# One of four weight sums of a seven-product scheme: added by DVE beside the product of one of its terms, in place of an accumulating DMA

## The chip, the cores and the metric

The kernel runs on one core of one Trainium2 chip. The metric is the device time in microseconds (us) from start to end of one execution; the median of three runs stands for the kernel. Engines are named as the profile names them: PE (matrix products), PEld (its weight loads), DVE, ACT, POOL, and SP, which only issues DMAs.

## The reference

The reference is a two-layer encoder trunk on x of 256 tokens by 2048 channels in float32. Each layer normalises x, projects it by `w_in`, runs three token mixers (retention, pooling, windowed attention), and merges their outputs with gates:

```
ya = (mixer a * silu gate) @ w_ret     # likewise yb @ w_pool, yc @ w_att, each 1024 -> 2048
gates = sigmoid(h @ w_in[mg])          # 3 x 2048 columns
merged = gates[0]*ya + gates[1]*yb + gates[2]*yc
x = x + merged @ w_out
```

What the change touches is the right half (columns 1024 to 2047) of the three products by `w_att`, `w_ret` and `w_pool`.

## The kernel before

All matrix products run in float32 split in two parts: each weight tile (128x1024 float32, 512 KB) is loaded into a `raw` tile by SP (line 258; 4 buffers), ACT casts it to `whi` (line 271; 4 buffers), DVE subtracts to get the rest, `wlo` (line 282; 3 buffers), and PE makes three products: a_hi by whi, a_hi by wlo, a_lo by whi. One tile so treated is a use. `_plan` writes all uses (some 660) down in the order in which PE takes them, and `weights()` issues the casts and subtractions two to three uses ahead and the loads up to four raw tiles ahead of the last `wlo`. A full use is 12 matmuls with 512 columns on PE.

A merge branch (`merge_branch`; three in each layer, six in all, numbered 1 to 6 here) walks over 40 full uses (`MERGE_STD`): gate columns in blocks 2, 3 and 0, then the left part of the output weight, block 0 (n = 25 to 28), then gate block 1 (n = 29 to 36), then weight block 1. After the use with number n in the table `AFTER` it puts in one of seven products, P1, P2, Q5, P6, Q3, P7, Q4, by which the right half, a two by two block product in rows, columns and channels, is made from seven block products and not eight. Each has two half uses, q = 0 and 1, of 6 matmuls each (line 893), into one of two PSUM banks (`px` for P1, P6, P7, Q4 and `pv` for P2, Q5, Q3). The right operands are quarters of the output weight or sums of them. Four products take sums:

- P1, Q5, P6 and Q4 walk through a chain: one tile for each q, to which POOL adds the next quarter by an accumulating DMA (line 284) after each use.
- P7 takes quarter (0,1) plus quarter (1,1). SP loads quarter (0,1) into a fresh raw tile, and POOL issues an accumulating DMA of quarter (1,1) on top of it (line 260). The cast to `whi` waits for that. Quarter (1,1) is also, unsummed, the operand of Q3, three uses earlier in `AFTER`.

After each product the result is copied aside by ACT (`snap`, line 867) or combined by DVE into the `mrg` tiles (`part`, `mg`, `mrg`, lines 810 to 828). In branches 3 and 6 PE also transposes finished `mrg` tiles (`pmt`, line 458) between the uses of gate block 1.

The order of instructions on an engine is set by the tile framework's scheduler, from the order of the program text and the buffers. On each engine instructions run in that order.

Of the kernel before, what the change touches and what calls it, by code (L numbers as in the profile page):

```python
# [12 lines left out]
ALU = mybir.AluOpType  # L13
# [3 lines left out]
P = 128  # L17
# [20 lines left out]

MERGE_STD = (("mg", 2), ("mg", 3), ("mg", 0), ("w", 0), ("mg", 1), ("w", 1))
BRANCHES = ((2, "w_att"), (0, "w_ret"), (1, "w_pool"))  # L40
AFTER = {12: "P1", 14: "P2", 17: "Q5", 23: "P6", 26: "Q3", 29: "P7", 34: "Q4"}


def _plan():


    tiles, uses = [], []

    def tile_no(name, l, rows, c0, w):
        tiles.append((name, l, rows, c0, w))  # L50
        return len(tiles) - 1

    def n_tiles(name, l, c0, nk):
        return [(name, l, [k2 * 256, k2 * 256 + P], c0, 512) for k2 in range(nk // 2)]

    def t_tiles(l, c0):
        return [("w_in", l, [(k4 * 4 + i) * P for i in range(4)], c0, 256) for k4 in range(KD // 4)]

    def use(ts):
        uses.extend(("tile", tile_no(*t)) for t in ts)  # L60

    def pool_tiles(l, g2):
        use([("pool_w", l, [g2 * 512 + i * P for i in range(4)], 0, 256)])

    def merge(l, b, name, late_pool):

        quarter = {}
        for i in range(2):
            for j in range(2):
                for q in range(2):  # L70
                    quarter[i, j, q] = tile_no(name, l, [(4 * q + 2 * kk + i) * P for kk in range(2)], 1024 + 512 * j, 512)
        n = 0
        for what, c in MERGE_STD:
            ts = n_tiles("w_in", l, OFF["mg"] + b * D + c * 512, KD) if what == "mg" else n_tiles(name, l, c * 512, KW)
            for t in ts:
                use([t])
                n += 1
                for q in range(2) if n in AFTER else ():
                    stage = {"P1": 0, "Q5": 1, "P6": 2, "Q4": 3}
                    prod = AFTER[n]  # L80
                    if prod in stage:
                        st = stage[prod]
                        uses.append(("chain", (l, b, q), st, quarter[((0, 0), (0, 1), (1, 1), (1, 0))[st] + (q,)],
                                     None if st == 3 else quarter[((0, 1), (1, 1), (1, 0))[st] + (q,)]))
                    elif prod == "P7":
                        uses.append(("sum", quarter[0, 1, q], quarter[1, 1, q]))
                    else:
                        uses.append(("tile", quarter[1, 0 if prod == "P2" else 1, q]))
            if what == "mg" and c == 2 and late_pool:
                pool_tiles(l, 1)  # L90

    for l in range(DEPTH):
        use(n_tiles("w_in", l, OFF["akv"], KD))
        for j in range(2):
            use(n_tiles("w_in", l, OFF["aq"] + j * 512, KD))
        for j in range(4):
            use(t_tiles(l, OFF["ag"] + j * 256))
        for h in range(RH):
            use(t_tiles(l, OFF["rq"] + h * RD) + t_tiles(l, OFF["rk"] + h * RD))
        for part in ("rv", "rg"):  # L100
            for j in range(2):
                use(n_tiles("w_in", l, OFF[part] + j * 512, KD))
        merge(l, *BRANCHES[0], False)
        for g in range(4):
            use(t_tiles(l, OFF["pv"] + g * 256))
        for g in range(4):
            use(t_tiles(l, OFF["pg"] + g * 256))
            if g == 2:
                pool_tiles(l, 0)
        merge(l, *BRANCHES[1], True)  # L110
        merge(l, *BRANCHES[2], False)
        for c in range(4):
            use(n_tiles("w_out", l, c * 512, KD))
    return tiles, uses
# [39 lines left out]
def kernel(  # L154
# [18 lines left out]
    nc = tc.nc  # L173
# [8 lines left out]
    def nm(s):  # L182
        uid[0] += 1
        return f"{s}_{uid[0]}"
# [46 lines left out]
    tiles, uses = _plan()  # L231
# [4 lines left out]
    def tile_of(n):  # L236
        _, _, rows, _, w = tiles[n]
        return [P, len(rows), w], weight_tiles[n].rearrange("p (k e) -> p k e", k=len(rows))

    def load_to(n):  # L240
        while len(raws) < min(n, len(uses)):
            i = len(raws)
            kind = uses[i][0]
            if kind == "chain":
                _, key, stage, no, _ = uses[i]
                if stage == 0:
                    shape, src = tile_of(no)
                    chains[key] = slot(shape, F32, "chain")
                    nc.sync.dma_start(out=chains[key], in_=src)
                raws.append(chains[key])  # L250
                continue
            shape, src = tile_of(uses[i][1])
            raw = wp.tile(shape, F32, tag="raw", name=nm("raw"), bufs=N_RAW)
            if i == 0:
                for k in range(shape[1]):
                    nc.sync.dma_start(out=raw[:, k], in_=src[:, k])
            else:
                nc.sync.dma_start(out=raw, in_=src)
            if kind == "sum":
                nc.gpsimd.dma_start(out=raw, in_=tile_of(uses[i][2])[1], accum_op=ALU.add)  # L260
            raws.append(raw)

    def hi_to(n):
        while len(his) < min(n, len(uses)):
            i = len(his)
            hi = wp.tile(list(raws[i].shape), F32R, tag="whi", name=nm("whi"), bufs=N_HI)
            if i == 0:
                for k in range(hi.shape[1]):
                    nc.vector.tensor_copy(hi[:, k], raws[i][:, k])
            else:  # L270
                nc.scalar.copy(hi, raws[i])  # L271
            his.append(hi)
# [14 lines left out]
    def weights():  # L287

        i = used[0]
        used[0] += 1  # L290
        ahead = min(i, 1) if i < 6 else N_LO - 1
        hi_to(i + ahead + 1)
        lo_to(i + ahead + 1)
        load_to(len(los) + N_RAW)
        hi_to(i + ahead + (1 if ahead < N_LO - 1 else 2))
        return his[i], los[i]
# [256 lines left out]
    for l in range(DEPTH):  # L553
# [305 lines left out]
        def merge_branch(which, ut, late_pool=None):  # L859
# [11 lines left out]
                    merged[c] = slot([P, 2, 512], F32, "mrg")  # L871
                done[c, t] = start(corner_task(first, c, t, gates, op, a, b))

            def product(name):
                if name == "P1":
                    state["x"] = bank("m0", "px")
                if name in ("P2", "Q5"):
                    state["v"] = bank("m1", "pv")
                acc_ = state["x"] if name in ("P1", "P6", "P7", "Q4") else state["v"]
                fresh = name in ("P1", "P2", "Q5")  # L880
                for q in range(2):
                    hi, lo = weights()
                    for kk in range(2):
                        j = 2 * q + kk
                        if name in ("P1", "P2", "Q4"):
                            i, t = {"P1": (0, 0), "P2": (1, 0), "Q4": (1, 1)}[name]
                            u = need(ut[j])
                            a = [u[:, i, h, t * P:(t + 1) * P] for h in range(2)]
                        else:
                            u = need(combos[j])  # L890
                            a = [u[:, ("Q5", "P6", "P7", "Q3").index(name), h] for h in range(2)]
                        for n, (ah, w) in enumerate(((a[0], hi), (a[0], lo), (a[1], hi))):
                            nc.tensor.matmul(acc_, lhsT=ah, rhs=w[:, kk], start=fresh and q == 0 and kk == 0 and n == 0,  # L893
                                             stop=q == 1 and kk == 1 and n == 2, skip_group_check=not fresh)
                if name == "P1":
                    snap("p1", acc_)
                elif name == "P2":
                    corner(2, 0, ALU.add, acc_, snaps["p1"])
                elif name == "Q5":
                    snap("q5", acc_)  # L900
                elif name == "P6":
                    snap("u2", acc_)
                elif name == "Q3":
                    corner(3, 0, ALU.subtract, acc_, snaps["u2"])
                elif name == "P7":
                    snap("u3", acc_)
                    corner(3, 1, ALU.subtract, snaps["q5"], snaps["u3"])
                else:
                    corner(2, 1, None, acc_, None)

            def between():
                state["n"] += 1
                if state["n"] == COMBOS_AT:
                    combos.extend(start(combos_task(j, ut, combos)) for j in range(4))
                if state["n"] in AFTER:
                    product(AFTER[state["n"]])

            for what, c in MERGE_STD:
                if what == "mg":
# [233 lines left out]
```

## Time and profile before

| | us |
|---|---|
| median of 3 runs | 1833.59 (1832.61 to 1835.93) |
| profiled execution | 1830.8 |
| its span | 1829.0 |
| PE busy in it | 1800.4 |
| DVE busy | 1206.9 |
| ACT busy | 917.6 |
| mean granted PE clock | 0.995 of full speed |

PE is busy in 98% of the span. The ends of matmuls in the profile are modelled and overlap, so the distance between the starts of two matmuls is the better measure of what one takes. The interval of the span not covered by PE is 28.6 us.

### The profile page before, as it was taken

How to read it: one execution, taken by the hardware profiler on the slowest of the kernel's cores; microseconds unless marked ns; L12 is line 12 of the kernel's file. 1: busy time of each engine (PE TensorE's matmuls, PEld its weight loads, DVE VectorE, ACT ScalarE, POOL GpSimd, SP SyncE). 2: the span in 40 equal slices, each digit the busy share in tenths (PEclk: the TensorE clock that was granted, in tenths of full speed). 3: DMA queues.
4: the chain of work that ended last, by engine and by line, in shares of the span. 5: the costliest groups of instructions: out<-in, count | busy, mean ns of one | idle time of the engine just before them, and what ended most of it. 6: DMA issues, size and time to landing. Idle time of an engine off the chain costs nothing.

```text
span 1829.0 us, 23536 instructions
## 1 busy us (share of the span) xinstructions
PE 1800.4 (98%) x8794; PEld 1512.3 (83%) x8794; DVE 1206.9 (66%) x1554; ACT 917.6 (50%) x1171; POOL 60.2 (3%) x70
## 2 busy tenths in 40 slices
PE   9999999999999999999999999999999999999999
PEld 7888888887888878878888888888878888788787
DVE  6778765755777666655567778657657776765654
ACT  6455554554445544544444555545544455444442
POOL 0000000000000000000000000000100000001000
PEclk9999999999999999999999999999999999999999
DMA  9554455586556876865565544556865568768654
GB/s 318 196 196 161 158 166 184 185 251 208 187 200 200 242 225 207 232 188 176 185 196 184 188 163 160 172 177 204 233 207 191 200 207 231 229 211 232 188 194 150
DMA packets 103011, 364.99 MB, mean 200 GB/s; under 512 B 11888, under 2 KB 12528, under 8 KB 102896
## 3 DMA queue, kind: packets, MB, share of 16 engines
q1 hardware_dynamic: 95264, 337.37, 54.9%
q0 software_dynamic: 6912, 25.17, 7.7%
q8 instruction: 69, 1.13, 0.2%
q10 hardware_dynamic: 720, 0.94, 0.2%
q14 instruction: 46, 0.38, 0.1%
HBM read 361.34 MB, written 2.10 MB: 199 GB/s over the span
## 4 chain that ended last, share of the span: by engine, by line
PE 92%; DMA 5%; issue 1%; DVE 1%; ACT 0%; ACTq 0%; SPq 0%; DVEq 0%; POOLq 0%
PE pn L384 58%; PE pt L430 16%; PE pt L433 8%; DMA raw<-in_weight_tiles_dram 4%; PE px L893 4%; PE pv L893 2%; DVE wlo L282 1%; ACT whi L271 0%; DMA xt<-in_x_t_dram 0%; PE pmt L458 0%; PE ppt L458 0%; PE pqt L458 0%; PE py L465 0%; PE pro L465 0%; PE pss L465 0%
## 5 line engine op out<-in xcount | busy, mean ns | idle before, releaser
L282 DVE TENSOR_TENSOR wlo<-raw,whi 128x1024 fp32r<-128x1024 f32 x615 | 750.8, 1223 | 492.3 <-PE pn L384 302.6
L271 ACT CAST whi<-raw 128x1024 fp32r<-128x1024 f32 x615 | 645.6, 1052 | 649.4 <-PE pn L384 364.7
L384 PE MATMUL pn<-whi,ht 128*128 128x512 f32 x2424 | 751.6, 391 | 0.8 <-ACT ht L483 0.5
L384 PEld LDWEIGHTS pn<-whi,ht 128*128 128x128 f32 x2424 | 454.8, 188 | 95.2 <-ACT ht L483 0.9
L384 PE MATMUL pn<-wlo,ht 128*128 128x512 f32 x1212 | 460.4, 390 | 1.2 <-DVE wlo L282 1.1
L430 PE MATMUL pt<-ht,whi 128*128 128x512 f32 x1280 | 449.5, 396 | 0.0
L433 PE MATMUL pt<-ht,wlo 128*128 128x256 f32 x1280 | 353.2, 281 | 0.0
L430 PEld LDWEIGHTS pt<-ht,whi 128*128 128x128 f32 x1280 | 238.6, 188 | 53.5
L384 PEld LDWEIGHTS pn<-wlo,ht 128*128 128x128 f32 x1212 | 228.0, 188 | 48.7 <-DVE wlo L282 2.3
L433 PEld LDWEIGHTS pt<-ht,wlo 128*128 128x128 f32 x1280 | 241.5, 189 | 3.2
L384 PE MATMUL pn<-whi,mt 128*128 128x512 f32 x512 | 158.4, 392 | 0.0
L384 PEld LDWEIGHTS pn<-whi,mt 128*128 128x128 f32 x512 | 96.1, 188 | 19.9
L384 PE MATMUL pn<-wlo,mt 128*128 128x512 f32 x256 | 97.0, 389 | 0.0
L282 DVE TENSOR_TENSOR wlo<-chain,whi 128x1024 fp32r<-128x1024 f32 x48 | 58.7, 1224 | 47.4 <-PE pn L384 39.9
L271 ACT CAST whi<-chain 128x1024 fp32r<-128x1024 f32 x48 | 50.7, 1056 | 52.8 <-PE pn L384 50.3
L384 PEld LDWEIGHTS pn<-wlo,mt 128*128 128x128 f32 x256 | 48.1, 188 | 9.7
L284 POOL DMA_DIRECT2D chain<-in_weight_tiles_dram x36 | 31.6, 877 | 736.3 <-DVE wlo L282 697.6
L893 PE MATMUL px<-whi,uo 128*128 128x512 f32 x96 | 37.7, 452 | 13.9 <-ACT whi L271 13.9
L448 ACT COPY tb<-pt 128x512 f32<-128x512 f32 x40 | 23.4, 585 | 54.5 <-PE pt L430 54.3
L924 ACT ACTIVATE mg<-pn,rstd 128x512 f32<-128x512 f32 x48 | 30.4, 686 | 37.1 <-PE pn L384 37.1
L384 PE MATMUL pn<-whi,utr 128*128 128x512 f32 x128 | 39.1, 389 | 0.0
L384 PE MATMUL pn<-whi,uta 128*128 128x512 f32 x128 | 39.1, 389 | 0.0
(216 smaller groups left out, 1458.1 us busy)
## 6 DMA issues: line engine op xcount, KB each, us to landing
raw<-in_weight_tiles_dram SPq DMA_DIRECT2D x615, 512.0 KB, 3.4
chain<-in_weight_tiles_dram POOLq DMA_DIRECT2D x36, 512.0 KB, 5.4
chain<-in_weight_tiles_dram SPq DMA_DIRECT2D x12, 512.0 KB, 4.3
raw<-in_weight_tiles_dram POOLq DMA_DIRECT2D x12, 512.0 KB, 8.9
xa<-in_x_dram SPq DMA_DIRECT2D x4, 512.0 KB, 6.6
out_dram<-o SPq DMA_DIRECT2D x7, 256.0 KB, 4.7
xt<-in_x_t_dram SPq DMA_DIRECT2D x5, 256.0 KB, 6.1
lag<-in_c_lag_dram SPq DMA_DIRECT2D x2, 512.0 KB, 4.6
```

Source lines behind the costliest of these rows:

```text
L271: nc.scalar.copy(hi, raws[i])
L282: nc.vector.tensor_sub(lo, raws[i], his[i].bitcast(F32))
L284: nc.gpsimd.dma_start(out=raws[i], in_=tile_of(uses[i][4])[1], accum_op=ALU.add)
L384: nc.tensor.matmul(pt[t] if early else pt[:, t, :], lhsT=a2[:, kk, ai, ts], rhs=w[:, kk], start=k2 == 0 and n == 0, stop=k2 == n2 - 1 and ...
L430: nc.tensor.matmul(pt[:, e, :], lhsT=hi[:, kk, es], rhs=a.rearrange("p h n -> p (h n)"), start=start, stop=stop)
L433: nc.tensor.matmul(pt[:, e, 0:S], lhsT=lo[:, kk, es], rhs=a[:, 0, :], start=False, stop=False)
L448: nc.scalar.copy(b, pt[:, :, S:2 * S])
L893: nc.tensor.matmul(acc_, lhsT=ah, rhs=w[:, kk], start=fresh and q == 0 and kk == 0 and n == 0, stop=q == 1 and kk == 1 and n == 2, skip_gr ...
L924: nc.scalar.activation(g, pt[:, t], AF.Sigmoid, scale=sc(t))
```

## The change

Q3 and P7 both come after n = 27, and their half uses alternate: Q3 q0, P7 q0, Q3 q1, P7 q1. P7 still loads quarter (0,1) into a fresh raw tile, but in place of the accumulating DMA DVE adds to it the raw tile of the use just before, which is the Q3 half use with the same q and holds quarter (1,1). That makes 12 DVE additions of 128x1024 float32 and 12 fewer accumulating DMAs of 512 KB in the whole kernel (two for each of six branches). The number of matmuls, casts and subtractions is the same. What followed each of the two products (copy, combination) follows both.

```diff
-AFTER = {12: "P1", 14: "P2", 17: "Q5", 23: "P6", 26: "Q3", 29: "P7", 34: "Q4"}
+AFTER = {12: ("P1",), 14: ("P2",), 17: ("Q5",), 23: ("P6",), 27: ("Q3", "P7"), 34: ("Q4",)}
...
                     elif prod == "P7":
-                        uses.append(("sum", quarter[0, 1, q], quarter[1, 1, q]))
+                        uses.append(("sum", quarter[0, 1, q]))
...
                 nc.sync.dma_start(out=raw, in_=src)
-            if kind == "sum":
-                nc.gpsimd.dma_start(out=raw, in_=tile_of(uses[i][2])[1], accum_op=ALU.add)
             raws.append(raw)
...
             hi = wp.tile(list(raws[i].shape), F32R, tag="whi", name=nm("whi"), bufs=N_HI)
+            if uses[i][0] == "sum":
+                nc.vector.tensor_tensor(raws[i], raws[i], raws[i - 1], ALU.add)
             if i == 0:
...
-                if state["n"] in AFTER:
-                    product(AFTER[state["n"]])
+                names = AFTER.get(state["n"], ())
+                for q in range(2):
+                    for name in names:
+                        half_product(name, q)
+                for name in names:
+                    product_done(name)
```

`half_product` is the body of the old `product` for one q; `product_done` is its tail (copy or combination).

On DVE in branch 1, before: raw_3688 and raw_3706 are Q3's tiles, raw_3718 is n = 27, raw_3732 is n = 28, raw_3756 is n = 29, raw_3774 is P7's q0 (its q1 follows three rows on).

```order
L282 TENSOR_TENSOR wlo_3730<-raw_3669,whi_3720 128x1024
L282 TENSOR_TENSOR wlo_3754<-raw_3688,whi_3734 128x1024
L282 TENSOR_TENSOR wlo_3772<-raw_3706,whi_3758 128x1024
L282 TENSOR_TENSOR wlo_3791<-raw_3718,whi_3777 128x1024
L282 TENSOR_TENSOR wlo_3804<-raw_3732,whi_3796 128x1024
L282 TENSOR_TENSOR wlo_3817<-raw_3756,whi_3808 128x1024
L828 TENSOR_TENSOR part_3835<-pv_3571,u_726_3728 128x512
L810 TENSOR_TENSOR mrg_3816<-part_3835,mg_3547 128x512
L282 TENSOR_TENSOR wlo_3838<-raw_3774,whi_3821 128x1024
```

The same place now: raw_3688 is n = 27, raw_3706 and raw_3732 are Q3's tiles, raw_3718 and raw_3756 are P7's, raw_3774 is n = 28.

```order
L281 TENSOR_TENSOR wlo_3730<-raw_3669,whi_3720 128x1024
L281 TENSOR_TENSOR wlo_3754<-raw_3688,whi_3734 128x1024
L265 TENSOR_TENSOR raw_3718<-raw_3718,raw_3706 128x1024
L281 TENSOR_TENSOR wlo_3772<-raw_3706,whi_3758 128x1024
L265 TENSOR_TENSOR raw_3756<-raw_3756,raw_3732 128x1024
L281 TENSOR_TENSOR wlo_3791<-raw_3718,whi_3776 128x1024
L281 TENSOR_TENSOR wlo_3809<-raw_3732,whi_3795 128x1024
L281 TENSOR_TENSOR wlo_3822<-raw_3756,whi_3813 128x1024
L281 TENSOR_TENSOR wlo_3834<-raw_3774,whi_3826 128x1024
```

Each addition stands in DVE's row one place ahead of the subtraction of the half use before its own. The second stands ahead of two subtractions, `wlo_3791` and `wlo_3809`, that do not need it.

On DVE in branch 3, before, from the combination of Q3 (`part_6695`) to that of P7 (`part_6785`), with the two `mrg_3752` rows that finish the left block 0:

```order
L828 TENSOR_TENSOR part_6695<-pv_6433,u_1277_6590 128x512
L812 TENSOR_TENSOR mg_6409<-part_6695,mg_6409 128x512
L813 TENSOR_TENSOR mrg_3816<-mrg_3816,mg_6409 128x512
L282 TENSOR_TENSOR wlo_6699<-raw_6635,whi_6681 128x1024
L812 TENSOR_TENSOR mg_6610<-pn_6614,mg_6610 128x512
L812 TENSOR_TENSOR mg_6612<-pn_6614,mg_6612 128x512
L282 TENSOR_TENSOR wlo_6718<-raw_6654,whi_6703 128x1024
L813 TENSOR_TENSOR mrg_3752<-mrg_3752,mg_6610 128x512
L282 TENSOR_TENSOR wlo_6736<-raw_6667,whi_6722 128x1024
L282 TENSOR_TENSOR wlo_6748<-raw_6679,whi_6740 128x1024
L813 TENSOR_TENSOR mrg_3752<-mrg_3752,mg_6612 128x512
```

The same place now, where wlo_6721 is of n = 30 and wlo_6748 of n = 31:

```order
L827 TENSOR_TENSOR part_6739<-pv_6433,u_1277_6590 128x512
L281 TENSOR_TENSOR wlo_6721<-raw_6672,whi_6711 128x1024
L811 TENSOR_TENSOR mg_6409<-part_6739,mg_6409 128x512
L827 TENSOR_TENSOR part_6743<-q_1254_6458,u_1305_6719 128x512
L812 TENSOR_TENSOR mrg_3858<-mrg_3858,mg_6409 128x512
L811 TENSOR_TENSOR mg_6411<-part_6743,mg_6411 128x512
L281 TENSOR_TENSOR wlo_6748<-raw_6685,whi_6725 128x1024
L812 TENSOR_TENSOR mrg_3858<-mrg_3858,mg_6411 128x512
L811 TENSOR_TENSOR mg_6610<-pn_6614,mg_6610 128x512
L811 TENSOR_TENSOR mg_6612<-pn_6614,mg_6612 128x512
L812 TENSOR_TENSOR mrg_3752<-mrg_3752,mg_6610 128x512
L812 TENSOR_TENSOR mrg_3752<-mrg_3752,mg_6612 128x512
```

The combination of P7 has moved ahead of the last four rows, which finish `mrg_3752`.

On PE in branch 3, before, from the end of P7 to the first transpose of `mrg_3752`:

```order
L893 MATMUL px_6264<-wlo_6718,uo_6383 128x512
L893 MATMUL px_6264<-whi_6703,uo_6383 128x512
L384 MATMUL pn_6717<-whi_6722,ht_144 128x512
...
L384 MATMUL pn_6717<-wlo_6736,ht_144 128x512
L384 MATMUL pn_6717<-whi_6722,ht_144 128x512
L458 MATMUL pmt_6780<-ident,mrg_3752 128x128 x4
```

The same place now:

```order
L891 MATMUL px_6264<-wlo_6683,uo_6383 128x512
L891 MATMUL px_6264<-whi_6674,uo_6383 128x512
L383 MATMUL pn_6614<-whi_6687,utp_5215 128x512
...
L383 MATMUL pn_6747<-whi_6699,ht_134 128x512 x4
...
L383 MATMUL pn_6747<-wlo_6721,ht_144 128x512
L383 MATMUL pn_6747<-whi_6711,ht_144 128x512
L457 MATMUL pmt_6784<-ident,mrg_3752 128x128 x4
```

The transpose stands after the matmuls of n = 30 in both. Before, one full use lay between the last matmul of P7 and it, now three do (n = 28, 29 and 30).

## Rows read from the trace of the kernel before

**Rows 1.** The page: busy time of each engine over the span.

```profile
PE 1800.4 (98%) x8794; PEld 1512.3 (83%) x8794; DVE 1206.9 (66%) x1554; ACT 917.6 (50%) x1171; POOL 60.2 (3%) x70
```

**Rows 2.** Groups by shape: count, busy us, mean ns, idle ahead and its releaser.

```profile
L893 PE MATMUL px<-whi,uo 128*128 128x512 f32 x96 | 37.7, 452 | 13.9 <-ACT whi L271 13.9
L893 PE MATMUL pv<-whi,uo 128*128 128x512 f32 x96 | 31.5, 389 | 0.0
...
L893 PE MATMUL px<-wlo,uo 128*128 128x512 f32 x48 | 22.5, 469 | 6.3 <-DVE wlo L282 6.3
```

**Rows 3.** Chain that ended last, branch 1, Q5 to Q4: start, length, what.

```profile
380.59 2.72 PE pv L893 x12
...
399.63 2.72 PE px L893 x12
...
411.63 3.18 DMA raw<-in_weight_tiles_dram
...
415.43 8.80 DMA raw<-in_weight_tiles_dram
...
441.72 2.72 PE px L893 x12
```

**Rows 4.** Same chain, branches 2 to 6: start of Q5, then of Q4.

```profile
608.37 2.72 PE pv L893 x12
...
671.45 2.72 PE px L893 x12
...
742.17 2.72 PE pv L893 x12
...
807.71 2.72 PE px L893 x12
...
1290.89 2.72 PE pv L893 x12
...
1352.62 2.72 PE px L893 x12
...
1519.27 2.72 PE pv L893 x12
...
1580.68 2.72 PE px L893 x12
...
1651.40 2.72 PE pv L893 x12
...
1715.93 2.72 PE px L893 x12
```

**Rows 5.** Same chain, branch 3 behind P7: two uses with a transpose block between.

```profile
796.31 2.75 PE pn L384 x12
799.50 8.21 PE pn L384 x36
```

**Rows 6.** Stretch of P7 in branch 3: length, busy and count by engine, PE clock.

```profile
786.00:792.00 6.00, 5.02 (x11) 3.61 (x12) 5.53 (x7) 4.21 (x5) 0.00 (x0) 0.55 0.40 131
```

**Rows 7.** The page's DMA issues: queue, count, size, median us to landing.

```profile
raw<-in_weight_tiles_dram SPq DMA_DIRECT2D x615, 512.0 KB, 3.4
...
raw<-in_weight_tiles_dram POOLq DMA_DIRECT2D x12, 512.0 KB, 8.9
```

**Rows 8.** Line 258's four loads behind P6: branch 1 (395:408), then branch 2 (622:636).

```profile
DMA to landing us min/median/max: 3.2/4.1/4.2
...
DMA to landing us min/median/max: 4.6/4.8/4.9
```

**Rows 9.** DVE in order of time, branch 1: start, length, idle ahead and its releaser.

```profile
404.94 1.23 DVE L282 TENSOR_TENSOR wlo<-raw,whi 128x1024 fp32r<-128x1024 f32 x1 [1.50 <-PE pn L384]
...
414.24 0.68 DVE L828 TENSOR_TENSOR part<-pv,u 128x512 f32<-128x512 f32 x1
```

**Rows 10.** The page's costliest groups: DVE's subtraction and ACT's cast.

```profile
L282 DVE TENSOR_TENSOR wlo<-raw,whi 128x1024 fp32r<-128x1024 f32 x615 | 750.8, 1223 | 492.3 <-PE pn L384 302.6
L271 ACT CAST whi<-raw 128x1024 fp32r<-128x1024 f32 x615 | 645.6, 1052 | 649.4 <-PE pn L384 364.7
```

More of the change, by code (lines that the diff above doesn't have):

```diff
@@ L77, in merge @@
                 n += 1
-                for q in range(2) if n in AFTER else ():
+                for q, prod in [(q, prod) for q in range(2) for prod in AFTER.get(n, ())]:
                     stage = {"P1": 0, "Q5": 1, "P6": 2, "Q4": 3}
-                    prod = AFTER[n]
                     if prod in stage:
@@ L872, in corner, with half_product @@
                 done[c, t] = start(corner_task(first, c, t, gates, op, a, b))
-            def product(name):
-                if name == "P1":
+            def half_product(name, q):
+                if name == "P1" and q == 0:
                     state["x"] = bank("m0", "px")
-                if name in ("P2", "Q5"):
+                if name in ("P2", "Q5") and q == 0:
                     state["v"] = bank("m1", "pv")
@@ L880, in product @@
                 fresh = name in ("P1", "P2", "Q5")
[L881 to L894, printed above, removed]
+                hi, lo = weights()
@@ new lines, in half_product @@
+                for kk in range(2):
+                    j = 2 * q + kk
+                    if name in ("P1", "P2", "Q4"):
+                        i, t = {"P1": (0, 0), "P2": (1, 0), "Q4": (1, 1)}[name]
+                        u = need(ut[j])
+                        a = [u[:, i, h, t * P:(t + 1) * P] for h in range(2)]
+                    else:
+                        u = need(combos[j])
+                        a = [u[:, ("Q5", "P6", "P7", "Q3").index(name), h] for h in range(2)]
+                    for n, (ah, w) in enumerate(((a[0], hi), (a[0], lo), (a[1], hi))):
+                        nc.tensor.matmul(acc_, lhsT=ah, rhs=w[:, kk], start=fresh and q == 0 and kk == 0 and n == 0,
+                                         stop=q == 1 and kk == 1 and n == 2, skip_group_check=not fresh)
@@ L895, in product, with product_done @@
+            def product_done(name):
+                x_, v_ = state["x"], state.get("v")
                 if name == "P1":
-                    snap("p1", acc_)
+                    snap("p1", x_)
                 elif name == "P2":
-                    corner(2, 0, ALU.add, acc_, snaps["p1"])
+                    corner(2, 0, ALU.add, v_, snaps["p1"])
                 elif name == "Q5":
-                    snap("q5", acc_)
+                    snap("q5", v_)
                 elif name == "P6":
-                    snap("u2", acc_)
+                    snap("u2", x_)
@@ L903, in product @@
                 elif name == "Q3":
-                    corner(3, 0, ALU.subtract, acc_, snaps["u2"])
+                    corner(3, 0, ALU.subtract, v_, snaps["u2"])
                 elif name == "P7":
-                    snap("u3", acc_)
+                    snap("u3", x_)
                     corner(3, 1, ALU.subtract, snaps["q5"], snaps["u3"])
                 else:
-                    corner(2, 1, None, acc_, None)
+                    corner(2, 1, None, x_, None)
             def between():
```

## The prediction

> **What bounds the kernel now.** I read the busy times first: PE is busy for 1800.4 of 1829.0 us and no other engine comes near [rows 1], so only time that PE loses can be won. Next I asked which groups of matmuls have idle time ahead of them. Nearly all of it stands before one kind: `px` from `uo`, the products P6 and P7, with 13.9 us waiting for ACT's cast and 6.3 us for DVE's subtraction. The `pv` products of the same shape wait for nothing [rows 2]. Then the chain that ended last, taken through one branch: PE runs without a gap from Q5 through P6, and then the chain leaves PE for a load of 3.18 us, an accumulating DMA of 8.80 us on top of it, a cast and a subtraction, and so reaches P7 [rows 3]. The median landing of those twelve DMAs on POOL's queue is 8.9 us, against 3.4 us for a plain load of the same 512 KB [rows 7].
>
> What P7 loses is read from starts, not from idle time. Between the starts of Q5 and P6 lie 84 matmuls in 19.04 us, 0.2267 us each [rows 3]. From the start of Q5 to that of Q4 there are 252 (Q5, P6, Q3 and P7 with 12 each, 17 full uses with 12 each), so 57.12 us without a wait. The chain has 61.13 us in branch 1 [rows 3], and 63.08, 65.54, 61.73, 61.41 and 64.53 us in branches 2 to 6 [rows 4]. In branches 3 and 6 two transpose blocks belong to it; two uses with one between are 3.19 us apart, not 2.72, so a block costs 0.47 [rows 5] and two 0.94. The excess is then 4.01, 5.96, 7.48, 4.61, 4.29 and 6.47 us: **32.8 us** in all, 1.8% of the time. It is more than the 20.2 us of idle time because PE comes back slow: in the stretch of P7 in branch 3 the granted clock was 0.55, that is, mostly the lower of its levels, 1.2 GHz, after the pause, and the matmuls of P7 last 452 and 469 ns on average where the same shape in `pv` lasts 389 [rows 2, 6].
>
> On which of the two to sum, the page Perfetto Trace Analysis of the Trainium skill (section Tensor Engine Instruction) says that the profiler records a matmul's start but estimates its end. The trace agrees: records of 389 ns follow each other every 227 ns. By idle time alone, the sum below would be 12.6 us higher.
>
> **The change, part by part.** *Removed: twelve accumulating DMAs.* The cast of P7 waited for load plus accumulation, 3.18 + 8.80 us and some 0.6 us between them [rows 3]; now it waits for a load and an addition. If nothing else is late, all 32.8 us go, the slow clock with them, since PE no longer pauses.
>
> *Added: twelve DVE additions* of 128x1024. None stands in the trace; the nearest row is DVE's subtraction of the same shape with two inputs, 1223 ns [rows 10]. I take 1.22 us, 14.7 us in all, on an engine with 622 us idle, so the sum counts zero if each lies in a gap. The cover must be looked at where it stands, since the second addition is ahead of two subtractions on DVE. On the clock of branch 1: the subtraction of n = 27 starts at 404.94, when PE has finished n = 24, and ends at 406.17 [rows 9]; it frees the buffer into which P7's q1 loads. Uses end at 407.63 (n = 25), 410.35 (26), 413.07 (27), and the four half uses, 1.36 us each, at 414.43, 415.79, 417.15 and 418.51. The load issued at about 406.2 is one of the four behind P6 that exist before the change too, and these landed in at most 4.2 us in branch 1 and 4.9 in branch 2 [rows 8]. So its data is there at 410.4 to 411.1, the addition ends by 412.3, the subtraction for P7 q0 queued behind it by 413.5, and PE wants that at its second matmul, 414.66. At least 1.1 us is left. The others each wait for PE to free a `wlo` buffer three uses back: they can end at 414.7 (Q3 q1), 415.9 (P7 q1) and 417.2 (n = 28), and are wanted at 416.0, 417.4 and 418.7. Casts of 1.05 us [rows 10] precede them and need a `whi` buffer four uses back, which is free earlier still. So four half uses in a row cost nothing, with 1.1 to 1.5 us in hand. The other end is a load as slow as the accumulating ones, 8.9 us [rows 7]: then the subtraction for P7 q0 is 2.9 us late in each branch, 17 us in all. I take zero, as the rows of the very loads are nearer; the accumulating traffic that made the far row is what goes away.
>
> *Moved: the combination of P7,* now ahead of the last rows that finish a `mrg` tile. In branches 3 and 6 PE transposes that tile right after n = 30, three full uses (8.16 us) after P7's end at 418.51, so at 426.67 in these coordinates. The load for n = 30 can start when Q3 q1's subtraction is done, about 414.5, and takes 3.4 [rows 7] to 4.9 us [rows 8]; after the cast and its own subtraction DVE stands at 420.2 to 421.7. Behind it are nine combination steps of at most 0.68 us [rows 9] and one subtraction, 7.3 us, so the tile is finished at 427.5 to 429.0, 0.8 to 2.3 us late. Back to back on DVE such steps may start closer, and then nothing is late. Between 0 and 2.3 us I take 1.0 us, twice, **2.0 us**. In the other four branches no matmul waits for these steps, and the subtractions behind them have two uses in hand.
>
> *Also moved: Q3 by one use, P7 by two,* with copies and PSUM banks as before; POOL's queue loses two entries a branch, and the chain's additions for Q4, issued after P6, keep seven full and four half uses (24 us) to land. No cost.
>
> **Sum.** 1830.8 (the profiled execution) - 32.8 + 2.0 = 1800.0 us. The median of the runs is 2.8 us over the profiled execution, and I add that: **1802.8 us**.
>
> **The rivals.** *Half uses starved in part.* Four half uses take four tiles in 5.44 us, where two full ones take two. If loads run a few us later than behind P6, each branch loses up to 2.9 us: 1809 to 1820 us. For it: loads, casts and subtractions are twice as dense there as anywhere else. Against it: what DVE and ACT do in that stretch fits with over a microsecond spare, and the loads in question were measured. 0.11.
>
> *Only the idle time comes back.* If the lower clock came from something else than the pause, 20.2 - 2.0 us would be won: 1815.4 us. Against it: the products `pv` in the same branches run at 389 ns [rows 2]. 0.03.
>
> *No gain.* If P7 waited for plain loads and not for the addition on top of them, the wait would come back in another place: 1833.6 us. The chain shows the accumulation itself for 8.80 of the 12 us, so 0.03.
>
> *Slower: DVE held by its second addition.* The wait that was ACT's alone is now DVE's, and all subtractions are queued behind it. With a landing of L us, the subtraction for P7 q0 is late by L - 6.0 us. From L = 11.5 us on, 5.5 us in each of six branches, the change loses; at 13 us it would be 7.0 us a branch, 1843 us. Nothing in the trace lands so late, not even the accumulating DMAs at 8.9 us. 0.02.
>
> **How the numbers follow.** The forecast has 0.81: 1799 to 1808 us, from the transposes' bounds (0 to 4.6 us) and the 2.8 us by which run and profile differ. With no new cost and no such difference it is 1798.0 us, the low end. The high end takes in a third of the starved case, 1.5 us a branch: 1812 us. Below 1798 I leave 0.03, above 1812 some 0.15. A measurement of this kernel tells about 0.2% (3.7 us) from no change. Faster than that: the forecast and the first two rivals, 0.95; within it 0.03; slower 0.02.
>
> **What would show it.** Right: no idle time before `px` from `uo`, mean durations of 389 ns in both its groups, Q5 to Q4 in 57.1 us in branches 1, 2, 4 and 5 and 58 to 60 in 3 and 6, and no accumulating DMA onto `raw`; DVE busy 14 to 15 us more; the additions with an idle time ahead of the second one that a load ended. A wait of PE's `pmt` rows for a `mrg` tile of about 1 us in branches 3 and 6 would bear out the second term. Wrong: idle time before `px` or `pv` that ends with DVE's subtraction (the starved case), matmuls still at 450 ns, or a new wait of PE in gate block 1 of other branches.

## The result, and the profile after

| | before | after |
|---|---|---|
| median, same chip | 1834.36 us (1832.61 to 1835.93, 4 runs) | 1802.39 us (1801.75 to 1803.41, 4 runs) |
| profiled execution | 1830.8 us | 1803.41 us |

The ratio is 0.9827, with a 95% interval of 0.9809 to 0.9844: the changed kernel is 32.0 us faster. The forecast was 1802.8 us, in a range of 1798 to 1812.

The page of the changed kernel (busy time of each engine; two rows of its DMA issues: count, size, median us to landing), which answers [rows 1, 7]:

```profile
PE 1792.2 (99%) x8794; PEld 1511.4 (84%) x8794; DVE 1218.9 (68%) x1566; ACT 919.3 (51%) x1171; POOL 49.7 (3%) x58
...
raw<-in_weight_tiles_dram SPq DMA_DIRECT2D x615, 512.0 KB, 3.4
chain<-in_weight_tiles_dram POOLq DMA_DIRECT2D x36, 512.0 KB, 5.5
```

The row of twelve accumulating DMAs onto `raw` is gone. Groups of PE by shape (count, busy us, mean ns, idle time ahead and its releaser), which answer [rows 2]; line 891 was 893, line 457 was 458:

```profile
L891 PE MATMUL px<-whi,uo 128*128 128x512 f32 x96 | 32.5, 389 | 0.0
...
L457 PE MATMUL pmt<-ident,mrg 128*128 128x128 f32 x64 | 9.3, 278 | 2.2 <-DVE mrg L812 2.1
L891 PE MATMUL px<-wlo,uo 128*128 128x512 f32 x48 | 18.7, 389 | 0.0
```

P6 and P7 wait for nothing now, and their matmuls last 389 ns like all others of that shape, where [rows 2] had 452 and 469. What is left is 2.2 us ahead of the transposes. The chain that ended last, branch 1, Q5 to Q4, which answers [rows 3]:

```profile
380.96 2.72 PE pv L891 x12
383.68 16.32 PE pn L383 x72
400.00 2.72 PE px L891 x12
402.72 10.88 PE pn L383 x48
413.60 1.36 PE pv L891 x6
414.96 1.36 PE px L891 x6
416.32 1.36 PE pv L891 x6
417.68 1.36 PE px L891 x6
419.04 19.04 PE pn L383 x84
438.08 2.72 PE px L891 x12
```

The chain no longer leaves PE: the four half uses follow each other every 1.36 us. From 380.96 to 438.08 are 57.12 us, the time of 252 matmuls without a wait. The same distance in all branches, as an excess over 57.12 us (58.06 in branches 3 and 6, with their transposes):

| excess, us, in branch | 1 | 2 | 3 | 4 | 5 | 6 | sum |
|---|---|---|---|---|---|---|---|
| before [rows 3, 4] | 4.01 | 5.96 | 7.48 | 4.61 | 4.29 | 6.47 | 32.8 |
| after | 0 | 0 | 3.77 | 0 | 0.34 | 0.92 | 5.0 |

The sum fell by 27.8 us, and the time of the profiled executions by 27.4. So the whole difference of these two executions lies in this stretch. The medians are 32.0 us apart because the median of before lies 3.6 us over its profiled execution and that of the changed kernel 1.0 us under its own. On DVE in branch 1, in order of time (start, length, idle ahead and its releaser), which answers [rows 9]:

```profile
405.31 1.23 DVE L281 TENSOR_TENSOR wlo<-raw,whi 128x1024 fp32r<-128x1024 f32 x1 [1.50 <-PE pn L383]
407.83 1.23 DVE L265 TENSOR_TENSOR raw<-raw,raw 128x1024 f32<-128x1024 f32 x1 [1.30 <-DMA raw<-in_weight_tiles_dram]
408.97 1.22 DVE L281 TENSOR_TENSOR wlo<-raw,whi 128x1024 fp32r<-128x1024 f32 x1
411.02 1.22 DVE L265 TENSOR_TENSOR raw<-raw,raw 128x1024 f32<-128x1024 f32 x1 [0.82 <-DMA raw<-in_weight_tiles_dram]
412.16 5.26 DVE L281 TENSOR_TENSOR wlo<-raw,whi 128x1024 fp32r<-128x1024 f32 x4
```

Both additions end an idle time that a load ended, 1.30 and 0.82 us, and four subtractions follow the second without a gap. PE never notices.

### The profile page after: what moved, and what is told of

The parts are those of the page before. It is cut to its first block, busy times and chain, and to the rows that moved or that the text cites. A ratio compares the mean times of both kernels' runs of the same rounds, so it can differ in the third digit from the quotient of the medians.

```text
span 1801.6 us, 23503 instructions
## 1 busy us (share of the span) xinstructions
PE 1792.2 (99%) x8794; PEld 1511.4 (84%) x8794; DVE 1218.9 (68%) x1566; ACT 919.3 (51%) x1171; POOL 49.7 (3%) x58
## 3 DMA queue, kind: packets, MB, share of 16 engines
q8 instruction: 69, 1.13, 0.3%
## 4 chain that ended last, share of the span: by engine, by line
PE 98%; DMA 1%; DVE 1%; issue 0%; ACT 0%; SPq 0%; DVEq 0%; ACTq 0%
PE pn L383 62%; PE pt L429 17%; PE pt L432 8%; PE px L891 3%; PE pv L891 3%; DMA raw<-in_weight_tiles_dram 1%; PE pmt L457 0%; PE ppt L457 0%; DVE wlo L281 0%; PE pn L389 0%; PE pqt L457 0%; PE py L464 0%; PE py L463 0%; PE pss L464 0%; PE pro L464 0%; PE pro L463 0%
## 5 line engine op out<-in xcount | busy, mean ns | idle before, releaser
L383 PE MATMUL pn<-whi,utr 128*128 128x512 f32 x128 | 39.1, 389 | 0.0
L383 PE MATMUL pn<-whi,utp 128*128 128x512 f32 x128 | 39.1, 389 | 0.0
L383 PE MATMUL pn<-whi,uta 128*128 128x512 f32 x128 | 39.1, 389 | 0.0
```

The lines of the kernel that those rows point to most:

```text
L383: nc.tensor.matmul(pt[t] if early else pt[:, t, :], lhsT=a2[:, kk, ai, ts], rhs=w[:, kk], start=k2 == 0 and n == 0, stop=k2 == n2 - 1 and ...
```

## The experiments

Three questions were open: which part of the old wait cost what, how much room the additions have, and what the 5 us are that came back in branches 3, 5 and 6. Times are medians; before was run on the same chip each time.

### What was removed: accumulation, series, bytes

**The new place alone.** Q3 and P7 alternate as in the changed kernel, but P7 keeps its accumulating DMA:

```diff
-                        uses.append(("sum", quarter[0, 1, q]))
+                        uses.append(("sum", quarter[0, 1, q], quarter[1, 1, q]))
...
+            if kind == "sum":
+                nc.gpsimd.dma_start(out=raw, in_=tile_of(uses[i][2])[1], accum_op=ALU.add)
...
-            if uses[i][0] == "sum":
-                nc.vector.tensor_tensor(raws[i], raws[i], raws[i - 1], ALU.add)
```

> The new place and the new order of Q3 and P7, but P7's sum still by an accumulating DMA on its raw tile; DVE adds nothing. Theory (the accumulating DMA made the wait): P7's two casts wait for load (4 us) and accumulation (8.8 us) again, 2 to 5 us a branch, 1815 to 1832 us. Rival (the new place made the gain): 1801 to 1805 us.

Measured: 1825.16 us (before 1831.07), ratio 0.9964, interval 0.995 to 0.9977. Waits of PE (us in total, times, longest), then the chain in branch 1:

```profile
PE px L891 <- DVE wlo L281: 7.9, 11, 0.8
PE px L891 <- ACT whi L270: 6.9, 6, 2.9
```

```profile
405.93 4.43 DMA raw<-in_weight_tiles_dram
...
410.98 6.12 DMA raw<-in_weight_tiles_dram
```

The wait of [rows 2] is still there, and the chain goes through the load and the accumulation as in [rows 3], though earlier. The excess is 25.2 us in sum. With the accumulating DMA kept, the place gave 5.9 us; the rest came with the addition.

**The old kernel with a plain second DMA.** POOL's DMA overwrites the tile and adds nothing (so P7 lacks one of its two terms); all else is the kernel before:

```diff
-                nc.gpsimd.dma_start(out=raw, in_=tile_of(uses[i][2])[1], accum_op=ALU.add)
+                nc.gpsimd.dma_start(out=raw, in_=tile_of(uses[i][2])[1])
```

> The kernel before, with POOL's second DMA onto P7's raw tile made a plain one that overwrites: P7 leaves one quarter out of its sum; bytes, queue and order of the DMAs stay. Theory (the accumulation itself is what takes 8.8 us): the second DMA lands in 3.5 to 5 us, P7 waits under 1 us a branch, 1799 to 1805 us. Rival (a second DMA in series through POOL's queue is the wait, whatever it does): 1825 to 1835 us.

Measured: 1816.12 us (before 1832.60), ratio 0.9906, interval 0.9892 to 0.9921. Neither expectation held: it lies halfway. The chain in branch 1, and the page's row for that DMA:

```profile
412.00 3.30 DMA raw<-in_weight_tiles_dram
...
415.95 6.86 DMA raw<-in_weight_tiles_dram
```

```profile
raw<-in_weight_tiles_dram POOLq DMA_DIRECT2D x12, 512.0 KB, 6.6
```

In the same place, on the same queue and with the same bytes, the plain DMA lands in 6.6 us where the accumulating one took 8.9 [rows 7]. The excess falls from 32.8 to 19.0 us. So without the adding 16.5 us of the median come back. The next run, which loads both terms through SP, is another 13.8 us faster. Whether those 13.8 us are the price of a second DMA that starts after the first, or of POOL's queue, no run separates: on that queue even the plain DMA took 6.6 us, where plain loads on SP's take 3.4 [rows 7]. The prediction's words "the accumulation itself for 8.80 of the 12 us" put both on the accumulation.

**Two loads side by side, added by DVE, at the old places.** `AFTER` and the code around it are those of before. P7 loads both terms through SP into two raw tiles, as many bytes as before, and DVE adds them:

```diff
+            if kind == "sum":
+                terms[i] = wp.tile(shape, F32, tag="raw", name=nm("term"), bufs=N_RAW)
+                nc.sync.dma_start(out=terms[i], in_=tile_of(uses[i][2])[1])
...
+            if i in terms:
+                nc.vector.tensor_tensor(raws[i], raws[i], terms.pop(i), ALU.add)
```

> The old places of Q3 (after n = 26) and P7 (after n = 29), and P7's sum by DVE from two plain loads into two raw tiles; the bytes loaded are those of the kernel before, and none is shared with Q3. Theory (only the accumulation was slow): P7 no longer waits or waits under 1 us a branch (two tiles for a half use in a ring of four), and the transposes of branches 3 and 6 wait for nothing; 1798 to 1808 us. Rival (the saved 6.3 MB of loads made the gain): 1825 to 1835 us.

Measured: 1802.34 us (before 1832.60), ratio 0.9834, interval 0.982 to 0.9849. The page's row for the added load, and PE's wait for P7:

```profile
term<-in_weight_tiles_dram SPq DMA_DIRECT2D x12, 512.0 KB, 4.6
```

```profile
PE px L897 <- DVE wlo L286: 2.0, 4, 0.6
```

The same gain without the new place and without saving a load. The 6.3 MB less to load that the change brings are not its cause: what counts is that both terms come by plain loads, side by side on SP's queue, and that DVE makes the sum. The excess is 4.1 us, spread over all branches, and the transposes wait 0.1 us in all.

### What was added: how much room DVE has

After each addition DVE does one, or three, further passes over the same tile (`max` of the tile with itself, which leaves its values as they are):

```diff
                 nc.vector.tensor_tensor(raws[i], raws[i], raws[i - 1], ALU.add)
+                for _ in range(1):
+                    nc.vector.tensor_tensor(raws[i], raws[i], raws[i], ALU.max)
```

> The changed kernel, with one more DVE instruction of 128x1024 (a maximum of the sum with itself, which changes nothing) behind each of the 12 additions, 1.22 us each. Theory (1.1 us or more in hand where the second addition stands): 0 to 0.3 us late a branch, 1802 to 1806 us. Rival (nothing in hand, each us of DVE there counts): 12 times 1.22 us or at least 6 times, 1810 to 1817 us.

Measured with one: 1802.64 us (before 1832.60), ratio 0.9837, interval 0.9822 to 0.9852. The groups of P7 and of the transposes:

```profile
L893 PE MATMUL px<-whi,uo 128*128 128x512 f32 x96 | 32.5, 389 | 0.0
...
L459 PE MATMUL pmt<-ident,mrg 128*128 128x128 f32 x64 | 9.3, 278 | 2.5 <-DVE mrg L814 2.5
```

Twelve more passes cost nothing before P7. They do not test the margin of 1.1 us for P7's q0, though, for the scheduler did not put both ahead of its subtraction. On DVE in branch 1, around the second addition:

```profile
411.65 1.23 DVE L265 TENSOR_TENSOR raw<-raw,raw 128x1024 f32<-128x1024 f32 x1
412.79 1.22 DVE L283 TENSOR_TENSOR wlo<-raw,whi 128x1024 fp32r<-128x1024 f32 x1
413.93 1.22 DVE L267 TENSOR_TENSOR raw<-raw 128x1024 f32<-128x1024 f32 x1
```

The subtraction at 412.79 is that for P7's q0. The second pass stands behind it, and the first one fell into the idle time before the second addition, so counted from the start of Q5 this subtraction is as early as in the changed kernel. Those for Q3's q1 and P7's q1 are 0.8 to 0.9 us later and PE waits for neither: that much of the 1.3 to 1.5 us which the prediction gave them is there.

> The same with three more DVE instructions of 128x1024 behind each addition, 3.7 us each. Theory (the subtractions queued behind the second addition come late once the 1.1 us are used up): DVE's subtraction for P7's q0 is about 5 us late in each branch, 1830 to 1845 us, the whole gain lost. Rival (PE is fed far enough ahead): below 1810 us.

Measured with three: 1834.15 us (before 1832.60), ratio 1.0007, interval 0.9994 to 1.0019. The groups of P7, PE's longest wait, and in branch 1 the rows of ACT that begin with the casts of P7's two halves:

```profile
L893 PE MATMUL px<-whi,uo 128*128 128x512 f32 x96 | 37.4, 442 | 11.2 <-ACT whi L272 11.2
...
L893 PE MATMUL px<-wlo,uo 128*128 128x512 f32 x48 | 21.6, 451 | 0.0
```

```profile
PE px L893 <- ACT whi L272: 11.2, 9, 2.1
```

```profile
413.38 2.00 ACT L272 CAST whi<-raw 128x1024 fp32r<-128x1024 f32 x2 [6.21 <-DVE raw L267]
419.33 3.89 ACT L272 CAST whi<-raw 128x1024 fp32r<-128x1024 f32 x4 [3.96 <-DVE raw L267]
```

The whole gain is lost. Some 3.4 us more of DVE in each of two places brings back the wait for the cast, and with it matmuls of 442 and 451 ns. The time is as expected, the mechanism is not. DVE's subtraction for P7's q0 was to come 5 us late, as in the rival "slower: DVE held by its second addition", but it came 2.8 us later, behind its own cast, and no `px` matmul waits for a subtraction (0.0). PE waits for the cast of the sum, which ACT starts when the last pass over the tile is done. The scheduler also interleaved the passes with the subtractions on DVE, and the matmuls of Q3 and P7 on PE, so this kernel differs from the changed one in more than the length of an addition. Between one and three passes the room ends; where, these two runs do not tell.

### What was moved: the transposes in branches 3 and 6

In branch 3 of the changed kernel the chain that ended last leaves PE behind P7; then PE in order of time, and a stretch behind the pause (length; busy and count of PE, PEld, DVE, ACT, POOL; PE clock; DMA share; GB/s):

```profile
766.34 5.50 DMA raw<-in_weight_tiles_dram
...
773.03 1.23 DVE wlo L281
774.25 0.60 DVE mg L811
...
776.66 1.14 DVE wlo L281
777.79 0.60 DVE mrg L812
...
780.11 0.69 DVE mrg L812
```

```profile
780.25 0.33 PE L457 MATMUL pmt<-ident,mrg 128*128 128x128 f32 x1 [1.44 <-DVE mrg L812]
780.85 0.55 PE L457 MATMUL pmt<-ident,mrg 128*128 128x128 f32 x3 [0.27 <-DVE mrg L812]
```

```profile
782.00:785.00 3.00, 3.00 (x9) 2.36 (x8) 1.67 (x2) 0.02 (x1) 0.00 (x0) 0.52 0.64 201
```

The load for n = 30 lands 5.50 us after its issue, its subtraction follows at 773.03, and behind that DVE does the rows of two `mrg` halves, P7's ahead of those that the transpose wants. PE loses 1.71 us of idle time, and then 3 us at a granted clock of 0.52, mostly the lower level.

Two edits of the changed kernel tell whether this order is the cause. First the same kernel again, for comparison.

> The changed kernel again, beside the kernel before and the variants below on one chip, as their base. Theory: 1801 to 1804 us, no idle time ahead of px from uo, and about 2 us of idle time ahead of the transposes pmt in branches 3 and 6. If the agreement of 1802.4 us was the chip's luck, the median moves by over 3 us here.

Measured: 1801.10 us (before 1831.07), ratio 0.9834, interval 0.9813 to 0.9854, with an excess of 1.86, 0.71 and 0.99 us in branches 3, 5 and 6.

**Transposes two uses later:**

```diff
-            yield 1 + j
+            yield (3 if c == 0 else 1) + j
```

> The changed kernel, with the transposes of left block 0 in branches 3 and 6 two uses later. Theory (the second term: PE waits there for DVE's moved combination, 3.8 and 0.9 us of excess with the slow clock after it in the profile of after): all six branches take 57.1 us from Q5 to Q4 (58.1 in 3 and 6 with the two transpose blocks), and the time falls by 3 to 5 us, to 1797.5 to 1800. Rival (the excess has another cause, such as late loads, and the wait only shows at the transposes): the wait moves to another matmul and the time stays at 1802 to 1803.

Measured: 1799.05 us, ratio 0.9823, interval 0.9803 to 0.9843; 2.05 us under the unchanged one, less than expected. The transposes wait for nothing, and branches 5 and 6 have no excess, but branch 3 keeps 1.13 us. Branch 5's 0.71 us were not won by this edit, which leaves the order on DVE there as it was: the subtraction ahead of the combination merely came 1.2 us earlier in this execution, after an earlier load. In branches 3 and 6 the edit won 1.7 us. PE's wait in it, and ACT in order of time (start, length, idle ahead and its releaser):

```profile
PE pn L383 <- DVE wlo L281: 0.8, 1, 0.8
```

```profile
772.03 1.05 ACT L270 CAST whi<-raw 128x1024 fp32r<-128x1024 f32 x1 [3.16 <-DMA raw<-in_weight_tiles_dram]
```

With the transposes out of the way, PE runs into a subtraction that stands behind the same combination rows on DVE. The load was late as well: the subtraction of n = 30 starts 41.2 us after Q5, where it started 40.3 us after it in the unchanged kernel.

**The combination of P7 four uses later:**

```diff
-            yield 1
+            yield 5 if c == 3 else 1
```

> The changed kernel, with the combinations of Q3 and P7 (column block 3) started four ticks later; on DVE three of their steps now stand behind the two rows that finish the left block 0, not ahead of them. Theory: about 1.9 us of DVE work leaves the way of the transposes, which waited 1.7 us in branch 3 and 0.4 in branch 6; the time falls by 2 to 5 us, to 1797.5 to 1800.5. Rival (not DVE's combination but something else holds the transposes): no change, 1802 to 1803.

Measured: 1798.30 us, ratio 0.9819, interval 0.9799 to 0.9839; 2.8 us under the unchanged one, as expected. Transposes still wait 0.4 us in all, and branch 3 keeps 0.82 us.

**Both edits together,** and the changed kernel beside them:

> The changed kernel with both edits: the transposes of gate block 1 come two uses later, and the combination of P7 waits five uses and not one. Theory A (the pmt wait of branches 3 and 6 is a race between the tile's last DVE steps and the transposes; each edit alone won 2.0 and 2.8 us of it): with both, pmt rows show no wait, Q5 to Q4 takes 58.1 us in branches 3 and 6 and 57.1 in the others, and the time is 2.5 to 4 us under the changed kernel run beside it, at 1797 to 1798.5 us. Rival B (a late load for n = 30 or 31 in branch 3 holds PE whatever comes behind it): about 1 us stays in branch 3, as it did with each edit alone (1.13 and 0.82 us), now ahead of a pn row and ended by DVE's wlo, and the time is no better than with the second edit alone, 2.5 to 3 us under the changed kernel.

> The changed kernel once more, unchanged, beside the run with both edits. By either theory 1801 to 1803 us, with 3 to 5 us of excess over 57.1 us (58.1 in branches 3 and 6) from Q5 to Q4, nearly all of it in branches 3, 5 and 6, and waits of PE's pmt rows for mrg of 1.5 to 2.2 us in sum.

Measured: 1797.94 us (1797.65 to 1798.37) with both and 1801.56 us (1800.92 to 1802.15) for the changed kernel; before 1833.76. The ratios to before are 0.9808 (0.9795 to 0.9822) and 0.9827 (0.9813 to 0.984). The chain of the kernel with both, branch 3:

```profile
731.72 2.72 PE pv L891 x12
...
769.80 13.61 PE pn L383 x60
783.41 0.43 PE pmt L457 x4
783.84 2.75 PE pn L383 x12
786.60 0.44 PE pmt L457 x4
787.03 2.77 PE pn L383 x12
789.81 2.72 PE px L891 x12
```

From 731.72 to 789.81 are 58.09 us, no wait is left, and the other branches have 57.12 and 58.09. The changed kernel beside it has an excess of 1.68, 1.16 and 0.73 us in branches 3, 5 and 6, 3.6 in sum, and the time differs by 3.6. So theory A holds. Rival B falls too, if not by this row alone: the subtraction of n = 30 in branch 3 starts 40.6 us after Q5, as late as in the changed kernel (40.1 to 40.6 in three profiles), but with either edit alone it started at 41.1 to 41.2. The subtraction of n = 32, for which PE waited with the first edit alone, now ends 1.5 us before PE wants it, so a load 0.6 us later would not have held PE. In branch 5 the subtraction ahead of the combination comes later than in any run of the changed kernel (39.8 us after Q5, against 38.7 to 39.5), and PE waits for nothing there. This version beats both kernels.

## Why the prediction was right, and where it was not

**The bound and the term removed: right.** P7 waited for a load with an accumulation behind it, and without them the 32.8 us are gone: branches 1, 2 and 4 run at 57.12 us to the hundredth, and `px` has no idle time. The slow matmuls went with the pause, so the rival "only the idle time comes back", 1815.4 us, fell. That the sum was made from starts and not from idle time decided 12.6 us. On ends and starts the prediction cited the Trainium skill, Perfetto Trace Analysis, section Tensor Engine Instruction, and this result agrees with it.

**One reason in it was too narrow.** The rival "no gain" was set aside because the accumulation takes 8.80 us in the chain. The plain DMA in the same place took 6.86 us there, and only half of the gain came with it. The other half came when P7's terms were loaded side by side through SP, and not in series with the second through POOL; how much of it is the series and how much the queue stays open.

**The additions at zero cost: right.** Each takes 1.226 us (1.22 were counted). The four loads behind P6 took 4.3, 5.0 and 5.3 us (least, median, most) in branch 1, a little over the 4.2 to 4.9 that were assumed, and the room was enough: in branch 1 the subtraction for P7's q0 ended 1.6 us before PE wanted it, where at least 1.1 us had been worked out. One extra pass cost nothing, three cost everything, but neither run puts the margin of that subtraction to the test. DVE's busy time rose by 12.0 us and not by 14 to 15. Records of DVE that follow without a wait overlap by some 0.08 us, so a fuller row has less busy time than its records have in sum; that this makes up the difference is argued and was not counted.

**The moved combination: mechanism right, term too small.** The term was 2.0 us for branches 3 and 6; the three profiles of the changed kernel have 5.0, 3.6 and 3.6 us. The wait in branch 3 was 1.71 us, inside its bounds of 0 to 2.3, but with two sizes off in opposite ways: the load for n = 30 took 5.50 us, not 3.4 to 4.9, and the combination steps start some 0.60 us apart, not 0.68. Two things were left out of the term. The first is the clock that fell after this pause in one profile: 3.77 us of excess came from 1.71 us of wait, the very effect that the prediction had just read in P7. (Where the clock stayed at 1.00, as in the first repeat, branch 3 still lost 1.86 us by 1.38 us of wait.) The second is branch 5, where "no matmul waits for these steps" failed: there PE waits for a subtraction behind the combination, for 0.3 to 1.2 us of excess, the more the later the subtraction ahead of the combination comes (38.7, 39.1 and 39.5 us after Q5 go with 0.34, 0.71 and 1.16 us).

**The difference between median and profile: did not carry over.** 2.8 us were added because the median of before lay so far over its profiled execution. For the changed kernel the profiled execution lies 1.0 us over the median. For profiled executions the forecast was 1800.0 and 1803.4 was measured, 3.0 of it from the term above. So the median came within 0.4 us because two small misses had opposite signs.

## What to carry to other kernels

Where a sum of two operands is made by an accumulating DMA and the consumer is starved, two plain loads and an addition on an engine with gaps can be cheaper than the DMA, as long as the addition's place in that engine's row has room. Extra passes of the same length can test the room, if the trace is read for where the scheduler put them. After such a gain look at what moved along: here rows in gate block 1 had been reordered, and two one-line edits to when they run gave back another 3.6 us. A wait on PE is to be priced from start to start, with the clock behind it, also where it is a small term.

## What the runs showed that was not expected

**The price of adding in the DMA.** 512 KB onto SBUF through POOL's queue: 8.9 us with addition, 6.6 without, in the same place, and POOL spends 870 and 552 ns to issue one. The figure belongs to the place: after n = 27, in the run with the new place alone, the accumulating one landed in 7.3 us, and the 36 onto `chain` in the changed kernel in 5.5. What sets the places apart stays open. The page DMA: Bandwidth & Descriptors of the Trainium skill gives a fit in its section Anatomy of one DMA (2.0 us plus the bytes over 436 GB/s); an estimate from it would be 3.2 us for this size, which agrees with none of these: the measurement decides.

**A pause and the clock.** In branch 3 PE's first transpose waited 1.44 us in one profile, and the clock fell to 0.52. In the kernel with one extra pass it waited about as long, and the clock stayed at 1.00 (PE in order of time, then a stretch behind it):

```profile
780.85 0.33 PE L459 MATMUL pmt<-ident,mrg 128*128 128x128 f32 x1 [1.37 <-DVE mrg L814]
```

```profile
782.00:785.00 3.00, 3.00 (x18) 2.46 (x16) 2.72 (x4) 0.81 (x2) 0.00 (x0) 1.00 0.48 158
```

What tells the two apart stays open.

**The spread.** On one chip 13 runs of before ranged over 10.1 us (1827.63 to 1837.76) and four of the changed kernel over 1.5. The mean granted clock went with it: 0.997 in the shortest of the 13 and 0.990 in the longest, 0.999 to 1.000 in the four. That the removed wait made the spread is argued, not shown.
